# Dilated stage of a hybrid attention block: first units queued by hand, weighing steps tied to other points of the order

## The chip, the cores and the metric

One core of one Trainium2 chip runs the whole kernel. Its engines work side by side and are tied by semaphores: PE (TensorE, matmuls; PEld is its weight load), DVE (VectorE), ACT (ScalarE), POOL (GpSimd) and SP (SyncE, which here only issues DMAs). The metric is the device time of one execution in microseconds (us).

## The reference, cut to what matters

```python
h = rms_norm(x, g_pre)                       # x: 1024 tokens x 1024 channels
a_qkv, bq, bk, bv, mq, ga, gb, gm, mg = jnp.split(h @ w_in, split_at, axis=-1)
aq, ak, av = rope(q), rope(k), v             # of a_qkv, 24 heads of 64 channels
for gi, (window, dil) in enumerate(((128, 1), (512, 4), (2048, 16))):
    o_g, lse_g = dilated_window_attention(aq[gi's 8 heads], ak[...], av[...], window, dil)
wts = softmax(stack(lses), axis=0)           # over the three groups
oa = einsum('gbsh,gbshd->bshd', wts, stack(outs))
...                                          # ob: grouped-query attention, om: attention into a memory
ya = (oa * silu(ga)) @ w_br_a                # yb, ym likewise
gates = sigmoid(mg + b_merge)                # 3 x 1024 channels
merged = gates[0] * ya + gates[1] * yb + gates[2] * ym
out = x + rms_norm(merged @ w_out, g_post)
```

The change touches the dilated attention (the loop over `gi`), the weighted sum `oa` over its three groups, and the place at which that sum's last part is worked out, which lies in the stage that makes the arguments of `gates`.

## The kernel before, in words

All large products are computed as three products of split operands: a tensor is split into a high part (`A.activation(dst_h, src, AF.Copy)` on ACT, line 105) and a low part (a subtraction on DVE, line 106), and PE multiplies high by high, low by high and high by low.

A *unit* is one weight slab of 1024x128: `load_w` loads it (SP, line 114, tile `wr`) and splits it into `wh` and `wl` (two buffers of each). `dense` then runs 48 matmuls in two halves of 24, over 512 tokens each (lines 143, 145, 147), and each half goes to one of two PSUM banks (`d`). The function `evac` of the unit empties the bank. `run_items` prepares unit n+1 before it runs unit n, and `weave` mixes the matmuls of units with pieces of attention, by costs. On PE the order is the order of the program. On the other engines a scheduler orders the instructions by priority and dependences, save between `manual.__enter__()` and `manual.__exit__()`, where they too stand in the order of the program.

The stages that the change touches come in this order.

- **Values**, up to about 582 us: the values of the dilated heads, queued by hand on ACT, DVE, POOL and SP; each result is added on DVE (line 911, tile `vr`), scaled on ACT and stored.
- **Dilated stage**, about 582 to 1020 us. There are 12 items (p, g), four pairs of heads p by three groups g, two units each (query and key). `rope_half` empties a bank on DVE: four multiplications by the sine table into `t2a`, one of the whole bank by the cosine table into `t1a` (line 1050 for queries, 1049 for keys), and POOL adds both into `aq` or `ak` (line 1056). `weave(3)` runs the first three units alone. Then each item runs `plan`: eight steps T = 0..7. At each, `soft(T)` does the masked minimum on DVE (line 1135) and the exponentials on ACT (lines 1138, 1140, 1143); PE transposes the results of an earlier T (lines 1160, 1169), ACT copies them to SBUF (line 1172, tile `app`), and PE multiplies them by the values (line 1186). Scores for T = 0..3 and for T = 4..7 are made in two batches (line 1123), so that DVE works in two bursts of four T. `stats` (PE line 1205) transposes and stores minima and sums.
- **Weighing.** Once the three items of a pair of heads p are done, `combine` gives five steps: `fetch` (reads the statistics back), `weights` (some ten small DVE instructions and one on ACT, lines 1314 to 1325, then DMAs that write the weights and read them back as `wgt`), and `weigh(0)`, `weigh(1)`, `weigh(2)`: a multiplication on DVE over 128x1024 (line 1334, tile `og`), for the second and third also an addition on POOL (line 1338), and for the third a store (SP, line 1340). For p = 0, 1, 2 they go into the items (p+1, 0) and (p+1, 1): `combining(T)` takes the next step when T is the entry for it in `STEP_T`. `tc.issue_after(fp["last"].ins)` keeps the step behind the last `soft` or rope of that point.
- **Block stage**, 1020 to 1240 us, queued by hand: 11 pairs of gate slabs, each by seven products of blocks (12 matmuls each, `prod`), with block sums on POOL (line 1432, `sf`), their splits (`ch`, lines 105 and 106), and evacuations on DVE (lines 1455 and 1461, the latter a multiplication of SBUF by SBUF) and ACT (1462). `slot(n, i)` is the work queued beside product i of pair n. For p = 3 the table `COM` puts the five weighing steps into slots.

Of the kernel before, what the change touches and what calls it, by code (L numbers as in the profile page):

```python
# [50 lines left out]
def block(ctx: ExitStack, tc: tile.TileContext, x, xT, memT, cst, msk, bcst, tabA, gpost,  # L51
# [111 lines left out]
    def run_items(count):  # L163
        for _ in range(count):
            n = done[0]
            prepare(n)
            prepare(n + 1)
            yield from queue[n][1](ready.pop(n))
            done[0] += 1

    def cost_items(count):
        return sum(q[2] for q in queue[done[0]:done[0] + count])

    def weave(count, att=None, att_cost=0.0, lead=1.0, prio=ATT_PRIO):
        dg = run_items(count)
        dc = cost_items(count)
        d = a = 0.0
        live_d, live_a = True, att is not None
        while live_d or live_a:
            if live_d and (not live_a or a / att_cost >= min(1.0, d / dc * lead)):  # L180
                try:
                    d += next(dg)
                except StopIteration:
                    live_d = False
                    d = 1e18
            else:
                try:
                    with tc.high_priority(offset=prio):
                        a += next(att)
                except StopIteration:  # L190
                    live_a = False
# [3 lines left out]
    def add_unit(src, evac):  # L195
        def gen(w):
            for half in range(2):
                p = psd()
                yield from dense(w, half, p)
                evac(half, p)  # L200
        queue.append((lambda: load_w(src), gen, UNIT))
# [251 lines left out]
    ET = mybir.EngineType  # L453
    manual = tc.manual_schedule(engines={ET.Activation, ET.DVE, ET.Pool})
# [383 lines left out]
    manual = tc.manual_schedule(engines={ET.Activation, ET.DVE, ET.Pool, ET.SP})  # L838
# [181 lines left out]
    with tc.tile_pool(name="aa", bufs=1, reuse_waits="tile") as aa:  # L1020
# [19 lines left out]
        def rope_half(o, half, p, scale, g):  # L1040

            t = slice(half * 512, half * 512 + 512)
            t1 = ab.tile([P, 512], F32, name="t1a", bufs=3)
            t2 = ab.tile([P, 512], F32, name="t2a", bufs=3)
            cos, sin = tab[0][:, t], tab[1][:, t]

            def mult(out, x, y):
                if scale is None:
                    return V.tensor_tensor(out, x, y, op=OP.mult)  # L1049
                return V.scalar_tensor_tensor(out, x, scale, y, op0=OP.mult, op1=OP.mult)  # L1050

            for a in range(4):
                i, j = slice(32 * a, 32 * a + 32), slice(32 * (a ^ 1), 32 * (a ^ 1) + 32)
                mult(t2[i], p[j], sin[j])
            fp["last"] = mult(t1, p, cos)
            G.tensor_tensor(half_of(o, half, g), classes(t1, g), classes(t2, g), op=OP.add)  # L1056

        def add_a(p_, g):
            base = (p_ * 3 + g) * 2
            d = OPS[p_, g] = {}  # L1060

            def qk_evac(name, scale):
                def evac(half, p):
                    if half == 0:
                        d[name] = ab.tile([P, S], F32, name=f"a{name}", bufs=2)
                    rope_half(d[name], half, p, scale, g)
                return evac

            add_unit(wu[base], qk_evac("q", -0.125))
            add_unit(wu[base + 1], qk_evac("k", None))  # L1070
# [166 lines left out]
        def joined(*pieces):  # L1237
            pieces = [x for x in pieces if x]
            return (lambda: [fn() for fn, _ in pieces]), sum(c for _, c in pieces)

        def plan(it, pre, nxt):

            out = []

            def combining(T):
                if todo and T == STEP_T[-len(todo)]:
                    with tc.issue_after(fp["last"].ins):
                        todo.pop(0)()

            def tokens(T):  # L1250
                if T >= 2:
                    for nm, k in late[:2]:
                        with tc.issue_after(fp["last"].ins):
                            split_block(nm, k)
                    del late[:2]
                if T == 5:
                    token_tiles("T1", [ab.tile([P, S], R, name=f"a{c}", bufs=2) for c in "qk"])
                    load_block("T1", (0, 1))

            def ready():  # L1260
                if pre and pre["key"][1] == 2:
                    todo.extend(combine(pre["key"][0], [OG.pop((pre["key"][0], x)) for x in range(3)]))

            if it and not pre:
                out.append(it["scores"][0])
            for T in range(NT if it else 4):
                if T == 2 and pre:
                    out += [(lambda: None, 300.0), pre["stats"]]
                if it:
                    out.append(it["soft"][T])  # L1270
                out.append((lambda T=T: combining(T), 0.0))
                if it and not nxt:
                    out.append((lambda T=T: tokens(T), 0.0))
                if T < 2:
                    if pre:
                        out.append(pre["trans"][T + 6])
                elif it:
                    out.append(it["trans"][T - 2])
                if T == 3:
                    out.append(joined(pre and pre["pv"][1], it and it["scores"][1]))  # L1280
                    if it:
                        out.append((it["values"], 0.0))
                    if pre and it:
                        out.append((ready, 0.0))
                if T == 7:
                    out.append(joined(it["pv"][0], nxt and nxt["scores"][0]))
            return out
# [78 lines left out]
        def token_tiles(nm, tiles):  # L1366
            TB.setdefault(nm, []).extend([t[:, half[x]] for x in range(2)] for t in tiles)

        def load_block(nm, ks=range(4)):
            for k in ks:  # L1370
                nc.sync.dma_start(TB[nm][k][1].bitcast(F32), tsd[int(nm[1]) - 1, k])

        def split_block(nm, k):
            h, l = TB[nm][k]
            split(h, l, l.bitcast(F32))
# [1 line left out]
        late = []  # L1377

        todo = []
        STEP_T = (4, 6, 0, 2, 5)  # L1380
        seq = [(p_, g) for p_ in range(4) for g in range(3)]
        add_a(*seq[0])
        add_a(*seq[1])
        weave(3)
        items = [item(*x) for x in seq] + [None]
        for n in range(len(seq)):
            if n + 2 < len(seq):
# [25 lines left out]
    manual = tc.manual_schedule(engines={ET.Activation, ET.DVE, ET.Pool, ET.SP})  # L1413
# [20 lines left out]
    def block_of(n, nm):  # L1434
        src = part(n, 3) if nm == "A22" else SF[int(nm[1]) - 1]
        t = sr.tile([P, 2, 512], R, name="ch", bufs=5)
        split(t[:, 0], t[:, 1], src)
        BL[n][nm] = t[:, 0], t[:, 1]
# [81 lines left out]

    pre = {}
    com = combine(3, [OG.pop((3, x)) for x in range(3)])
    COM = {(0, 0): 0, (1, 1): 1, (2, 1): 2, (3, 1): 3, (4, 1): 4}

    def slot(n, i):

# [11 lines left out]
        if n < last:  # L1538
# [7 lines left out]
            elif i == 5:  # L1546
                weight_sum(n + 1, 4)
                block_of(n + 1, "S2")
        if (n, i) in COM:
            com[COM[n, i]]()  # L1550
        if (n, i) == (5, 0):
# [305 lines left out]
```

## Time and profile before

| what | value |
|---|---|
| time, median of 3 runs | 1458.5 us (1457.19 to 1459.48) |
| profiled execution: time | 1458.88 us |
| profiled execution: span from first to last instruction | 1457.1 us |
| mean granted TensorE clock | 0.995 |
| instructions | 20924 |

The profile lists instructions with the time at which they start, their duration and, in brackets, how long their engine had been idle and which instruction released it. A wait for several things is put down to the one that came last. A matmul of 512 columns starts about 0.23 us after the one before it while the shown duration is 0.39 us, because matmuls are pipelined; so distances between starts are what is to be read for PE.

### The profile page before, as it was taken

The page shows a single profiled execution, that of the slowest core. Times are in us where ns is not written, and L with a number is a line of the kernel's source. Part 1 is how long each engine was busy: PE and PEld are TensorE (multiplying, and loading weights), DVE is VectorE, ACT ScalarE, POOL GpSimd, SP SyncE. Part 2 cuts the span into 40 slices and gives each one's busy share as a digit, 9 for nine tenths or more (in the row PEclk, how much of TensorE's full clock was granted, in tenths as well). Part 3 has the DMA queues.
Part 4 walks back from the last instruction along what each step waited for, and adds up shares of the span by engine and source line. Part 5 has one row for each costly group of instructions (what it writes and reads, how often), then busy time and mean ns, then how long its engine had stood idle before and what let it go on. Part 6 is the DMA issues. An engine that isn't in the chain of part 4 may idle for free.

```text
span 1457.1 us, 20924 instructions
## 1 busy us (share of the span) xinstructions
PE 1423.2 (98%) x7548; PEld 1140.9 (78%) x7548; DVE 984.5 (68%) x1739; ACT 641.8 (44%) x1441; POOL 499.7 (34%) x382
## 2 busy tenths in 40 slices
PE   8999999999999999899999999999999999999998
PEld 7899986565666888687777778778787888888887
DVE  7665468776762367586687686873788787659643
ACT  6543365665554243145444544463534434212221
POOL 1415504666664420132232242230334331035322
PEclk9999999999999999999999999999999999999999
DMA  6332012232112675412131241342443443767122
GB/s 239 100 116 73 17 64 91 80 105 73 62 44 72 237 222 173 122 43 57 47 90 59 57 113 51 89 145 81 139 156 134 173 173 108 272 219 273 48 92 101
DMA packets 99448, 168.05 MB, mean 115 GB/s; under 512 B 21968, under 2 KB 51856, under 8 KB 99344
## 3 DMA queue, kind: packets, MB, share of 16 engines
q1 hardware_dynamic: 80192, 148.76, 31.7%
q10 hardware_dynamic: 19152, 17.96, 3.7%
q8 instruction: 59, 0.97, 0.3%
q14 instruction: 45, 0.37, 0.1%
HBM read 124.38 MB, written 42.30 MB: 114 GB/s over the span
## 4 chain that ended last, share of the span: by engine, by line
PE 76%; DVE 9%; ACT 5%; issue 5%; POOL 3%; DMA 2%; SPq 0%; ACTq 0%; POOLq 0%; DVEq 0%
PE s L125 9%; PE sc L125 9%; PE d L145 9%; PE d L143 8%; PE d L147 8%; PE s L967 6%; PE sc L1705 5%; PE ov L754 3%; PE d L967 2%; PE s L738 2%; PE tr L720 2%; PE s L739 2%; PE d L535 1%; PE tr L1186 1%; PE s L1123 1%
## 5 line engine op out<-in xcount | busy, mean ns | idle before, releaser
L143 PE MATMUL d<-hh,wh 128*128 128x512 f32 x672 | 271.2, 404 | 7.6 <-DVE t1a L1050 5.8
L147 PE MATMUL d<-hh,wl 128*128 128x512 f32 x672 | 269.4, 401 | 0.0
L145 PE MATMUL d<-hl,wh 128*128 128x512 f32 x672 | 269.4, 401 | 0.0
L105 ACT ACTIVATE wh<-wr 128x1024 fp32r<-128x1024 f32 (+1 forms) x79 | 72.2, 917 | 222.1 <-PE d L145 125.8
L143 PEld LDWEIGHTS d<-hh,wh 128*128 128x128 f32 x672 | 127.5, 190 | 38.0 <-issue 10.6
L145 PEld LDWEIGHTS d<-hl,wh 128*128 128x128 f32 x672 | 127.3, 189 | 31.3 <-issue 8.4
L147 PEld LDWEIGHTS d<-hh,wl 128*128 128x128 f32 x672 | 127.4, 190 | 29.1 <-issue 4.7
L745 POOL TENSOR_TENSOR bl<-bl,bp 128x512 f32<-128x512 f32 x96 | 131.5, 1370 | 53.6 <-ACT bp L741 48.1
L125 PE MATMUL sc<-hh,wh 128*128 128x512 f32 x384 | 118.4, 389 | 0.0
L106 DVE TENSOR_TENSOR wl<-wr,wh 128x1024 fp32r<-128x1024 f32 x53 | 74.6, 1409 | 37.5 <-ACT wh L105 37.1
L1056 POOL TENSOR_TENSOR aq<-t1a,t2a 128x512 f32<-128x512 f32 x24 | 44.7, 1862 | 160.7 <-DVE t1a L1050 149.4
L721 DVE TENSOR_REDUCE bn<-tr 128x1 f32<-128x512 f32 x128 | 86.1, 686 | 17.4 <-PE tr L720 16.1
L1049 DVE TENSOR_TENSOR t2a<-d,tab 32x512 f32<-32x512 f32 x96 | 66.0, 687 | 47.2 <-PE d L147 41.9
L741 ACT ACTIVATE bp<-s 128x512 f32<-128x512 f32 x128 | 75.9, 595 | 46.8 <-PE s L739 45.7
L1056 POOL TENSOR_TENSOR ak<-t1a,t2a 128x512 f32<-128x512 f32 x24 | 55.4, 2308 | 117.8 <-DVE t1a L1049 91.9
L125 PEld LDWEIGHTS sc<-hh,wh 128*128 128x128 f32 x384 | 72.1, 188 | 15.0
L1050 DVE SCALAR_TENSOR_TENSOR t2a<-d,tab 32x512 f32<-32x512 f32 x96 | 66.0, 687 | 25.8 <-PE d L147 24.0
L1432 POOL TENSOR_TENSOR sf<-wr 128x512 f32<-128x512 f32 x22 | 29.7, 1368 | 145.1 <-DVE ch L106 71.7
L1636 POOL TENSOR_TENSOR acc<-acc,th 128x1024 f32<-128x1024 f32 x15 | 40.9, 2729 | 112.0 <-DVE th L1635 109.3
L125 PE MATMUL sc<-hl,wh 128*128 128x512 f32 x192 | 74.7, 389 | 0.0
L1143 ACT ACTIVATE pra<-pra,sts 128x128 f32<-128x128 f32 (+2 forms) x152 | 66.4, 438 | 17.0 <-DVE sts L1135 17.0
L1135 DVE CUSTOM_DVE_ANT_0 pra<-s,mask 128x192 f32<-128x192 f32 (+2 forms) x192 | 56.1, 348 | 15.7 <-PE s L1123 14.9
(375 smaller groups left out, 3435.4 us busy)
## 6 DMA issues: line engine op xcount, KB each, us to landing
wr<-in_wu SPq DMA_DIRECT2D x64, 512.0 KB
th<-thd SPq DMA_DIRECT2D x24, 512.0 KB
thd<-rs ACTq DMA_DIRECT2D x44, 256.0 KB
g2d<-fth SPq DMA_DIRECT2D x24, 256.0 KB
vdr<-vr ACTq DMA_DIRECT2D x24, 256.0 KB
wgt<-wgd SPq DMA_DIRECT2D x24, 256.0 KB
ot<-od SPq DMA_DIRECT2D x12, 512.0 KB
wr<-in_wbr SPq DMA_DIRECT2D x24, 256.0 KB
```

The source lines that it names most:

```text
L105: A.activation(dst_h, src, AF.Copy)
L106: V.tensor_tensor(dst_l, src, dst_h.bitcast(F32), op=OP.subtract)
L125: PE.matmul(out_ps, a, b, start=i == 0, stop=i == n - 1)
L143: PE.matmul(dst, wh[:, k, :], hh[k][:, t], start=k == 0, stop=False)
L145: PE.matmul(dst, wh[:, k, :], hl[k][:, t], start=False, stop=False)
L147: PE.matmul(dst, wl[:, k, :], hh[k][:, t], start=False, stop=k == 7)
L721: fp["last"] = V.tensor_reduce(st[i]["n"][:, j, c:c + 1], s, axis=AX.X, op=OP.min)
L741: A.activation(pp, s, AF.Exp, scale=-1.0)
L745: G.tensor_tensor(lsum[i % 2], lsum[i % 2], pp, op=OP.add)
L967: PE.matmul(now[j], a, b, start=k == 0 and q == 0, stop=k == end and q == 2)
L1056: G.tensor_tensor(half_of(o, half, g), classes(t1, g), classes(t2, g), op=OP.add)
L1705: PE.matmul(parts[h], *terms[h][j], start=j == 0, stop=j == 23)
```

## The change

```diff
             def combining(T):
-                if todo and T == STEP_T[-len(todo)]:
+                while todo and T == STEP_T[-len(todo)]:
                     with tc.issue_after(fp["last"].ins):
                         todo.pop(0)()
...
         todo = []
-        STEP_T = (4, 6, 0, 2, 5)
+        STEP_T = (4, 7, 3, 3, 7)
         seq = [(p_, g) for p_ in range(4) for g in range(3)]
         add_a(*seq[0])
         add_a(*seq[1])
+        manual = tc.manual_schedule(engines={ET.Activation, ET.DVE, ET.Pool, ET.SP})
+        manual.__enter__()
         weave(3)
+        manual.__exit__(None, None, None)
...
-    COM = {(0, 0): 0, (1, 1): 1, (2, 1): 2, (3, 1): 3, (4, 1): 4}
+    COM = {(0, 0): 0, (1, 4): 1, (2, 4): 2, (3, 4): 3, (4, 4): 4}
```

Three things change. The first three units of the dilated stage stand in the order of the program on ACT, DVE, POOL and SP too. Within the items, `weights` goes from T = 6 to T = 7, `weigh(0)` from T = 0 and `weigh(1)` from T = 2 both to T = 3, and `weigh(2)` from T = 5 to T = 7; `while` lets two steps share one T. In the block stage the last four steps go from slot 1 to slot 4 of their pairs. PE has the same 5711 rows in the same order. SP keeps its order but for one weight load that stands two rows earlier and one store that stands behind two loads, both near the end of the dilated stage.

DVE at the start of the dilated stage: `vr` are the last additions of the values, `wl<-wr,wh` is the split of a weight slab, `t2a` and `t1a` are the rope of a bank.

```order
 L911 TENSOR_TENSOR vr<-s_5701,vy_4879 128x512
 L911 TENSOR_TENSOR vr<-s_5702,vy_4880 128x512
-L106 TENSOR_TENSOR wl<-wr,wh 128x1024
 L1050 SCALAR_TENSOR_TENSOR t2a<-d,tab_4850 32x512 x4
 L1050 SCALAR_TENSOR_TENSOR t1a<-d,tab_4849 128x512
 L1050 SCALAR_TENSOR_TENSOR t2a<-d,tab_4850 32x512 x4
 L1050 SCALAR_TENSOR_TENSOR t1a<-d,tab_4849 128x512
+L106 TENSOR_TENSOR wl<-wr,wh 128x1024
 L1049 TENSOR_TENSOR t2a<-d,tab_4850 32x512 x4
 L1049 TENSOR_TENSOR t1a<-d,tab_4849 128x512
```

The split of the third unit's slab moves from ahead of the first unit's two ropes to behind them.

DVE in the first burst (T = 0..3) of an item (p+1, 1), before: `pra` is the masked minimum, `og` a weighing.

```order
L1334 TENSOR_TENSOR og<-og,wgt 128x1024
L1135 ISA pra,sts<-s_7288,mask 128x192
L1135 ISA sts 128x1
L1135 ISA pra,sts<-s_7289,mask 128x192
L1135 ISA sts 128x1
L1050 SCALAR_TENSOR_TENSOR t2a<-d,tab_4850 32x512
L1050 SCALAR_TENSOR_TENSOR t1a<-d,tab_4849 128x512
L1049 TENSOR_TENSOR t2a<-d,tab_4850 32x512 x4
```

The same place after:

```order
L1050 SCALAR_TENSOR_TENSOR t2a<-d,tab_4850 32x512
L1050 SCALAR_TENSOR_TENSOR t1a<-d,tab_4849 128x512
L1135 ISA pra,sts<-s_7291,mask 128x192
L1135 ISA sts 128x1
L1135 ISA pra,sts<-s_7292,mask 128x192
L1135 ISA sts 128x1
L1334 TENSOR_TENSOR og<-og,wgt 128x1024 x2
L1049 TENSOR_TENSOR t2a<-d,tab_4850 32x512 x4
```

The two weighings, which stood behind the minima of T = 0 and of T = 2, stand together behind those of T = 3 and behind the rest of a query rope. On ACT the copy `app` that stood behind the exponentials of T = 1 now stands behind one more pair of exponentials.

DVE in the block stage at pair 4, before (`ch` are splits, `rs` and `sp` evacuations):

```order
L106 TENSOR_TENSOR ch<-wr,ch 128x512
L106 TENSOR_TENSOR ch<-sf_9949,ch 128x512
L1334 TENSOR_TENSOR og<-og,wgt 128x1024
L1455 TENSOR_TENSOR rs<-s_10457,sp_9952 128x512
L1461 TENSOR_TENSOR rs<-rs,rb 128x512
L106 TENSOR_TENSOR ch<-sf_9946,ch 128x512
```

One pair after the change (lines of the program behind the inserted ones are numbered three higher):

```order
L106 TENSOR_TENSOR ch<-sf_9951,ch 128x512
L1334 TENSOR_TENSOR og<-og,wgt 128x1024
L1458 TENSOR_TENSOR sp_9958<-s_10520,sp_9956 128x512
L106 TENSOR_TENSOR ch<-sf_9950,ch 128x512
L1458 TENSOR_TENSOR rs<-s_10543,sp_9957 128x512
L1464 TENSOR_TENSOR rs<-rs,rb 128x512
```

The weighing stood between the splits of S4 and S1 of its own pair (operands of products 4 and 5); it now stands between the splits of S3 and S2 of the next pair (operands of its products 3 and 2). POOL's block sum for S4 of the next pair stands behind the addition of that weighing.

## The prediction

> **What bounds the kernel now.** I read the busy table first, then the list of PE's own waits, then the timelines around those waits, and for the block stage a table by pairs.
>
> ```profile
> PE   1423.2 (98%) x7548; PEld 1140.9 (78%) x7548; DVE 984.5 (68%) x1739; ACT 641.8 (44%) x1441; POOL 499.7 (34%) x382
> ...
> PE d L143 <- DVE t1a L1050: 5.8, 1, 5.8
> PE tr L1205 <- ACT app L1172: 4.4, 6, 1.1
> PE tr L1160 <- ACT app L1172: 2.8, 4, 1.6
> PE s L125 <- DVE ch L106: 1.7, 2, 0.9
> ```
>
> PE is the bound, and its order does not change. So the time can move only by what PE waits, or by what clock it gets. These four groups (total us, times, longest) add up to 14.7 us of idle PE, and all of them lie where the change touches. What is not among them the change cannot win; what it makes later can be lost.
>
> **The first units (5.8 us of idle, and a slow clock behind it).**
>
> ```profile
> 582.69 0.39 PE L143 MATMUL d<-hh,wh 128*128 128x512 f32 x1
> 593.34 0.39 PE L147 MATMUL d<-hh,wl 128*128 128x512 f32 x1
> 599.53 0.76 PE L143 MATMUL d<-hh,wh 128*128 128x512 f32 x1 [5.80 <-DVE t1a L1050]
> 603.46 0.39 PE L143 MATMUL d<-hh,wh 128*128 128x512 f32 x1
> ...
> 599.50:603.40 3.90, 3.87 (x9) 0.50 0.00 0
> ...
> 587.97 0.69 DVE L911 TENSOR_TENSOR vr<-s,vy 128x512 f32<-128x512 f32 x1 [0.93 <-DMA vdr<-vr]
> 594.63 1.23 DVE L106 TENSOR_TENSOR wl<-wr,wh 128x1024 fp32r<-128x1024 f32 x1 [5.97 <-ACT wh L105]
> 595.89 2.79 DVE L1050 SCALAR_TENSOR_TENSOR t2a<-d,tab 32x512 f32<-32x512 f32 x4
> 598.69 0.69 DVE L1050 SCALAR_TENSOR_TENSOR t1a<-d,tab 128x512 f32<-128x512 f32 x1
> ...
> 593.54 1.06 ACT L105 ACTIVATE wh<-wr 128x1024 fp32r<-128x1024 f32 x1 [2.40 <-PE d L145]
> ```
>
> Unit 0 runs from 582.69 to 593.34, first and last of 48 matmuls: 10.65 / 47 = 0.2266 us from start to start. Its first bank was full at 582.69 + 23 x 0.2266 + 0.39 = 588.3, and DVE was free at 587.97 + 0.69 = 588.7. But the next instruction on DVE was the split of unit 2, which needs `wh` from ACT, which overwrites a buffer that unit 0 reads until 593.5. So DVE stood 5.97 us, the rope came after it, and PE waited 5.80 us for a bank. Then it ran at a granted clock of 0.50 for 3.90 us (the row of that stretch: length, busy PE and count, clock). From 593.34 to 603.46 there are ten starts where 10 x 0.2266 = 2.27 us would do: 10.12 - 2.27 = **7.85 us lost**.
>
> With the split behind both ropes: the first rope takes 588.7 + 2.79 + 0.69 = 592.2, and PE asks for that bank at 593.6, spare 1.4 us. The second bank is full at 593.7, its rope ends at 597.2, and PE asks for it at 593.57 + 24 x 0.2266 = 599.0, spare 1.8. The split then takes 597.2 to 598.4 and its unit starts at 593.57 + 10.88 = 604.4, spare 6.0. Queued behind that split are the two ropes of unit 1, of which the first bank fills only at 599.0, and SP's load into the freed `wr`, 2.6 us later than before, for unit 4, whose split waits for the end of unit 2 at 593.57 + 2 x 10.88 = 615.3, 17 us after that load is issued. The ends: 5.8 if only the idle goes, 7.85 with the clock. I take 7.85, since without the idle nothing in these rows slows the clock.
>
> **First burst of items (p+1, 1), three times.**
>
> ```profile
> 751.52 2.01 DVE L1334 TENSOR_TENSOR og<-og,wgt 128x1024 f32<-128x1024 f32 x1
> 753.44 0.35 DVE L1135 CUSTOM_DVE_ANT_0 pra<-s,mask 128x192 f32<-128x192 f32 x1
> 754.55 1.97 DVE L1334 TENSOR_TENSOR og<-og,wgt 128x1024 f32<-128x1024 f32 x1
> 759.03 1.38 DVE L1049 TENSOR_TENSOR t2a<-d,tab 32x512 f32<-32x512 f32 x2 [0.54 <-POOL og L1338]
> ...
> 753.90 0.46 ACT L1143 ACTIVATE pra<-pra,sts 128x192 f32<-128x192 f32 x1 [1.22 <-DVE sts L1135]
> 755.07 0.57 ACT L1172 ACTIVATE app<-tr 128x512 f32<-128x512 f32 x1
> 755.55 0.39 ACT L1138 ACTIVATE pra<-pra,sts 128x128 f32<-128x128 f32 x1
> 756.27 0.44 ACT L1143 ACTIVATE pra<-pra,sts 128x192 f32<-128x192 f32 x1
> ...
> 755.70 0.28 PE L1205 MATMUL tr<-cs,sts 128*32 128x128 f32 x1 [1.14 <-ACT app L1172]
> ```
>
> A weighing of 2 us stands between the minima of T = 0 and T = 1, so ACT starves for 1.22 us, its copy `app` ends late, and PE waits 1.14. Taken out of the burst, the 1.22 go; but ACT now does one more pair of exponentials ahead of that copy, 755.55 to 756.27 = 0.72. Net 0.5 us earlier, three times: **1.5 us**. Ends: 0 and 3 x 1.14 = 3.4. Behind the double weighing on DVE waits the rope of the key's first half. Four minima take from 753.44 to 754.55, 0.28 each, so the burst, two minima ahead of 751.52, begins at 751.0. It holds eight minima and the rest of the query rope (two operations, 1.4), then two weighings: 751.0 + 2.2 + 1.4 + 3.9 = 758.5, which is not later than the 759.03 at which that rope starts now. POOL's addition moves from ahead of the query's last `aq` addition to behind it; the 0.54 goes. `weights` at T = 7 ends where it ended, since the same instructions stand ahead of its last one, and its reader comes 3 us later than now.
>
> **Second burst of the same items.**
>
> ```profile
> 770.51 2.79 DVE L1334 TENSOR_TENSOR og<-og,wgt 128x1024 f32<-128x1024 f32 x1
> 776.68 2.79 DVE L1050 SCALAR_TENSOR_TENSOR t2a<-d,tab 32x512 f32<-32x512 f32 x4
> 773.67 0.40 ACT L1138 ACTIVATE pra<-pra,sts 128x128 f32<-128x128 f32 x1 [1.02 <-DVE sts L1135]
> 775.37 0.55 PE L1160 MATMUL tr<-cs,pra 128*128 128x128 f32 x3 [0.51 <-ACT app L1172]
> ...
> 956.11 2.06 POOL L1056 TENSOR_TENSOR ak<-t1a,t2a 128x512 f32<-128x512 f32 x1 [1.61 <-DVE t1a L1049]
> 961.86 2.97 POOL L1056 TENSOR_TENSOR ak<-t1a,t2a 128x512 f32<-128x512 f32 x1 [3.69 <-DVE t1a L1049]
> 964.86 0.63 ACT L105 ACTIVATE t2a<-t2a 128x512 fp32r<-128x512 f32 x1 [3.22 <-POOL ak L1056]
> 968.42 0.55 PE L1160 MATMUL tr<-cs,pra 128*128 128x128 f32 x3 [1.61 <-ACT app L1172]
> ```
>
> In the first two groups ACT starves 1.02 us for minima behind `weigh(2)` and PE then waits 0.51; ACT's order is the same there, so both 0.51 go. In the third, ACT first stands behind a split that waits for POOL's `ak`, which took 2.97 beside the weighing and 2.06 without one: 0.9 of the 1.61. Together **1.9 us**; ends 0 and 2.6. Behind `weigh(2)` wait the rest of `stats` and the next query rope, which starts at 776.68; the same instructions stand ahead of it in both orders, so it starts no later.
>
> **Block stage.**
>
> ```profile
> 1118.73:1137.77 19.04, 15.78 (x22) 1.00 0.36 114
> ...
> sum 98.00, PE 96.35; mean PE 19.27
> ...
> 1107.89 2.02 DVE L1334 TENSOR_TENSOR og<-og,wgt 128x1024 f32<-128x1024 f32 x1
> 1110.55 2.39 DVE L1461 TENSOR_TENSOR rs<-rs,rb 128x512 f32<-128x512 f32 x1
> 1112.86 0.68 DVE L106 TENSOR_TENSOR ch<-sf,ch 128x512 fp32r<-128x512 f32 x1
> 1109.99 2.40 POOL L1338 TENSOR_TENSOR og<-og 128x1024 f32<-128x1024 f32 x1 [9.96 <-DVE og L1334]
> 1113.59 0.50 PE L125 MATMUL s<-aq,ch 128*128 128x512 f32 x1 [0.73 <-DVE ch L106]
> ...
> 1143.79 0.69 DVE L106 TENSOR_TENSOR ch<-sf,ch 128x512 fp32r<-128x512 f32 x1 [1.48 <-ACT ch L105]
> ```
>
> The first row is a pair without weighing: 19.04 us, of which DVE is busy 15.78. The sum is over the five pairs from 1039.77 to it, the other four with a step each: 98.00 - 5 x 19.04 = 2.8 us too long. At 1113 the split of S1 is late by a weighing and by the `rs` beside POOL's addition (2.39 where 0.69 is usual). In slot 4 the weighing (2.0) and one blocked operation (1.7) delay the next pair's S4 split by up to 3.7 us. In the pair from 1137.77 that split ends at 1144.48, and product 4 needs it at 1137.77 + 4 x 2.72 + 0.45 = 1149.1, spare 4.6: no wait. I take **2.3** of 2.8, since part of pair 1 is the start of the stage. Ends: a gain of 2.8 and a loss of 1.5, if half the spare is missing in two pairs.
>
> The Trainium skill speaks against this place. "SBUF — State Buffer", section "SBUF: two separate sides", says that DVE with two SBUF inputs and POOL share one port pair that the first to start holds for its whole instruction. The 2.39 beside 2.40 agrees. By that rule alone the weighing in slot 4, among POOL's sums, would stand blocked, and the block term would be that of rival 2.
>
> **The sum**, against the profiled execution of 1458.88 (span 1457.1 and 1.8 around it): 7.85 + 1.5 + 1.9 + 2.3 = 13.55, so 1445.3. The median shown is 0.4 lower; I say **1445.0 us**.
>
> **Rivals.**
>
> 1. *Only the first units pay.* ACT's exponentials stay the limit in the bursts, and PE's waits move by a few transposes without shrinking. For it: ACT's order gets worse in the first burst. Against it: the idle brackets name DVE. 1458.5 - 7.85 = 1450.7, and up to 1453 with small new waits.
> 2. *The weighing is blocked by POOL's sums* in slot 4: it waits for a sum as `og` at 770.51 did (2.79 where 2.0 is usual) or longer, up to the 2.4 of an addition, on top of 3.7. That is 6.1 against a spare of 4.6, so 1.5 us lost in each of three pairs: the block term turns from -2.3 to +1.7 (the 2.8 gone, 4.5 new). 1449.0.
> 3. *The hand queue does not help:* the first rope is held by something else than the split, such as the memory that it takes over from the values stage. The 7.85 stay: 1452.8. Against it: before, it followed the split with no idle at all, and only POOL, PE and DVE hold it.
> 4. *Slower:* in the block stage the delay does not die out within a pair, since DVE has only some 3 us to spare in 19, so each weighed pair and the three after it lose. To decide it must eat 13.55 + 2.9, some 2.3 us in each of seven pairs. For it: the busy DVE. Against it: the pair from 1118.73 follows a weighed one and takes 19.04.
>
> **How the numbers follow.** Chances: forecast 0.66 (its own range 1442 to 1448.5), rival 1 0.13, rival 2 0.09, rival 3 0.06, rival 4 0.03, no change 0.03. The range reaches from all upper gains (7.85 + 3.4 + 2.6 + 2.8 = 16.7, so 1441.8) over rivals 1 and 2 to 1452. About 0.2% (2.9 us) is what a measurement can tell from no change. Rivals 1 to 3 all stay faster than that: faster 0.94, same 0.03, slower 0.03.
>
> **What would show it.** In the profile after: no idle of PE behind the first unit and a clock of 1.00 there; the split of unit 2 behind two query ropes; PE's waits on `app` at L1205 near 0.6 in three items and at L1160 gone in two; block pairs of 19.0 to 19.2 us. I am wrong if a new wait of PE on `t1a`, or on `ch` at the first matmuls of products 2 to 4, stands in the list.

## The result, and the profile after

| | before | after |
|---|---|---|
| median of the runs | 1458.65 us | 1449.26 us |
| ratio, 95% interval | | 0.9936 [0.9919, 0.9954] |
| span of the profiled execution | 1457.1 us | 1448.1 us |

The kernel became 9.4 us faster; 13.5 were forecast, and 1449.26 lies inside the range but 0.8 above the likeliest case's own. The sum hides two errors and one term that is right to 0.03 us, so the span has to be cut. Four instants of PE do it: the first matmul of unit 0, the first transposition at L1205 that PE waits for, and the starts of pair 0 and pair 6 of the block stage. These are rows of PE of the kernel before and then of the changed one (the block pairs' rows stand further down).

```profile
582.69 0.39 PE L143 MATMUL d<-hh,wh 128*128 128x512 f32 x1
721.80 0.28 PE L1205 MATMUL tr<-cs,sts 128*32 128x128 f32 x1 [0.34 <-ACT app L1172]
```
```profile
582.01 0.39 PE L143 MATMUL d<-hh,wh 128*128 128x512 f32 x1
713.24 0.28 PE L1205 MATMUL tr<-cs,sts 128*32 128x128 f32 x1 [0.34 <-ACT app L1172]
```

Between the two rows lie 139.11 us before and 131.23 after. In the same way for the rest; each stretch holds the same matmuls in the same order in both kernels. Pair 0 of the block stage starts at 1020.22 before and 1009.87 after, pair 6 at 1137.77 and 1128.77.

| stretch | before | after | difference | forecast |
|---|---|---|---|---|
| ahead of unit 0 (order unchanged) | 582.69 | 582.01 | -0.68 | 0 |
| unit 0 to the first wait at L1205 ("first units") | 139.11 | 131.23 | **-7.88** | -7.85 |
| first wait at L1205 to pair 0 ("bursts") | 298.42 | 296.63 | **-1.79** | -3.4 |
| pair 0 to pair 6 ("block stage") | 117.55 | 118.90 | **+1.35** | -2.3 |
| from pair 6 on | | | 0.00 | 0 |

The -0.68 is no work of the change: in the other kernels below unit 0 starts at 581.2 to 582.3, and nothing there was moved. One execution of the kernel e6_later took 2370.49 us at a granted clock of 0.557 and is left out of that kernel's median below.

The list of PE's own waits after (total us, times, longest):

```profile
PE tr L1205 <- ACT app L1172: 3.7, 6, 0.9
PE tr L1160 <- ACT app L1172: 2.4, 5, 1.7
...
PE s L125 <- ACT ch L105: 1.7, 3, 0.7
```

The wait on `t1a` is gone. The waits on `app` have shrunk by 1.1 us instead of 3.4. The wait on `ch` is a new one: three times, and it names ACT, where the old one named DVE.

**First units.** DVE after, and a table of PE by stretches (length; busy us and count of PE, PEld, DVE, ACT, POOL; granted clock; DMA):

```profile
588.37 2.79 DVE L1050 SCALAR_TENSOR_TENSOR t2a<-d,tab 32x512 f32<-32x512 f32 x4
591.18 0.69 DVE L1050 SCALAR_TENSOR_TENSOR t1a<-d,tab 128x512 f32<-128x512 f32 x1
593.09 2.79 DVE L1050 SCALAR_TENSOR_TENSOR t2a<-d,tab 32x512 f32<-32x512 f32 x4 [1.22 <-PE d L147]
...
596.50 1.22 DVE L106 TENSOR_TENSOR wl<-wr,wh 128x1024 fp32r<-128x1024 f32 x1
...
592.00:603.00 11.00, 11.00 (x50) 9.13 (x49) 8.02 (x11) 1.06 (x1) 4.30 (x3) 1.00 0.42 115
```

The split at 596.50 now stands behind both query ropes. The first rope ends at 591.87, where 592.2 was worked out. PE is busy for all of the 11 us, at a clock of 1.00. Both parts of the term came: the 5.80 of idle and the 2.05 of the slow clock behind it.

**Block stage**, table by pairs, 3 to 6, after:

```profile
1068.22:1088.56 20.34, 19.61 (x85) 15.61 (x84) 17.12 (x20) 8.02 (x12) 6.66 (x5) 1.00 0.43 130
1088.56:1108.72 20.16, 19.61 (x86) 15.61 (x84) 16.95 (x19) 7.39 (x11) 8.88 (x5) 1.00 0.42 131
1108.72:1128.77 20.05, 19.59 (x85) 15.61 (x84) 16.82 (x20) 7.39 (x11) 9.89 (x6) 1.00 0.38 131
1128.77:1147.81 19.04, 19.04 (x85) 15.77 (x84) 14.56 (x18) 7.38 (x11) 7.02 (x5) 1.00 0.46 167
```

Pair 1, which held `weights` and took 20.51, takes 19.34 now, pair 2 19.06; pair 0 is 0.4 longer than before. But the three pairs behind a weighing, 3 to 5, take 20.0 to 20.3, and DVE (fourth column) is busy for 17 us in them.

The 1.35 is the difference of two executions, and not all of it belongs to the slots. Pair 0, where no weighing was moved, takes 19.17 to 19.95 in the traces of this document, and 19.95 and 19.96 in two kernels with the slots of before (e2_steps, e11_slot1); its 0.40, after a wait of 0.46 for `hl`, is not the slots' doing. Pairs 1 to 5 take 98.00 before and 98.95 after. In four more traces with the slots of before they take 97.99 to 98.28 (e1_queue, e2_steps, e3_slot1, e11_slot1), in one more with the new slots 98.47 (e4_weights6). So the new slots cost some 0.2 to 1.0 us where a gain of 2.3 was forecast.

### The profile page after: what moved, and what is told of

The parts are those of the page before. It is cut to its first block, busy times and chain, and to the rows that moved or that the text cites. A ratio compares the mean times of both kernels' runs of the same rounds, so it can differ in the third digit from the quotient of the medians.

```text
span 1448.1 us, 20924 instructions
## 1 busy us (share of the span) xinstructions
PE 1420.2 (98%) x7548; PEld 1138.7 (79%) x7548; DVE 986.6 (68%) x1739; ACT 642.2 (44%) x1441; POOL 500.4 (35%) x382
## 4 chain that ended last, share of the span: by engine, by line
PE 78%; DVE 6%; ACT 5%; issue 4%; POOL 3%; DMA 3%; ACTq 0%; SPq 0%; POOLq 0%; DVEq 0%
PE d L145 9%; PE sc L125 9%; PE d L147 9%; PE d L143 9%; PE s L125 8%; PE s L967 6%; PE sc L1708 5%; PE ov L754 3%; PE tr L1186 2%; PE d L967 2%; PE s L1123 2%; PE s L738 2%; PE tr L720 2%; PE s L739 2%; PE d L535 2%
```

## Where the block stage lost

Rows of all engines of the changed kernel, around pair 3 (starts at 1068.22) and pair 4 (1088.56), in order of time:

```profile
1063.71 3.52 POOL L1435 TENSOR_TENSOR sf<-wr 128x512 f32<-128x512 f32 x2 [13.99 <-DMA wr<-in_wu]
...
1068.95 3.11 DVE L1334 TENSOR_TENSOR og<-og,wgt 128x1024 f32<-128x1024 f32 x1
...
1077.67 0.71 ACT L1465 ACTIVATE rs<-rs,hbm 128x512 f32<-128x512 f32 x1
1079.32 1.14 ACT L105 ACTIVATE ch<-sf 128x512 fp32r<-128x512 f32 x2
1079.99 0.50 PE L125 MATMUL s<-hh,ch 128*128 128x512 f32 x1 [0.73 <-ACT ch L105]
1080.71 0.30 PEld L125 LDWEIGHTS s<-hh,ch 128*128 128x128 f32 x2 [0.43 <-DVE ch L106]
...
1090.12 2.40 POOL L1338 TENSOR_TENSOR og<-og 128x1024 f32<-128x1024 f32 x1 [2.57 <-DVE og L1334]
1090.56 2.51 DVE L106 TENSOR_TENSOR ch<-sf,ch 128x512 fp32r<-128x512 f32 x1
1092.48 1.75 POOL L1435 TENSOR_TENSOR sf<-wr,sf 128x512 f32<-128x512 f32 x1
1094.25 4.79 SPq L1350 DMA_DIRECT2D wr<-in_wu  x2
```

Product 4 of pair 3 wants S4's first half from ACT and gets it late, 0.73 us, and then waits again for the second half from DVE, 0.43. ACT's copy stands behind the `tanh` of the pair before (and one evacuation), and these wait for DVE's `rs`, which is queued behind the weighing. That weighing took 3.11 among POOL's sums; the other two took 2.02. POOL's addition held a split of 0.7 for 2.51, as the prediction had it. One path more shows in the last two rows: POOL's last sum ends at 1094.23 (1092.48 + 1.75), and SP's load of the next `wr` goes out at 1094.25, because that sum frees its memory. The sum itself was not what S4 waited for in pair 4: it is S4's own, and ACT's copy of it began at 1099.48, over 5 us after its end. But an addition in front of the sum delays a load too, and POOL's next sums (`13.99 <-DMA wr` in the first row) wait for such a load.

How late DVE runs is read off one instruction: the start of its split of S4, counted from the start of the pair. These are its first and last rows of pairs 1 to 5 of the kernel before, and then its rows in pairs 1, 3 and 6 after:

```profile
1050.48 0.69 DVE L106 TENSOR_TENSOR ch<-sf,ch 128x512 fp32r<-128x512 f32 x1 [1.46 <-ACT ch L105]
...
1127.35 0.69 DVE L106 TENSOR_TENSOR ch<-sf,ch 128x512 fp32r<-128x512 f32 x1 [1.48 <-ACT ch L105]
```
```profile
1040.55 0.69 DVE L106 TENSOR_TENSOR ch<-sf,ch 128x512 fp32r<-128x512 f32 x1 [1.48 <-ACT ch L105]
...
1079.97 0.69 DVE L106 TENSOR_TENSOR ch<-sf,ch 128x512 fp32r<-128x512 f32 x1 [1.48 <-ACT ch L105]
...
1136.64 0.69 DVE L106 TENSOR_TENSOR ch<-sf,ch 128x512 fp32r<-128x512 f32 x1 [1.48 <-ACT ch L105]
```

Less the starts of their pairs, with the same reading of three experiments (in the last, pair 4's split shows no wait in front of it):

| start of S4's split in pair | 1 | 2 | 3 | 4 | 5 | 6 |
|---|---|---|---|---|---|---|
| before | 10.71 | 8.57 | 7.91 | 8.63 | 8.62 | 6.02 |
| after | 10.73 | 10.42 | 11.75 | 11.57 | 11.48 | 7.87 |
| later pairs (e6_later) | 10.72 | 10.39 | 9.19 | 9.12 | 10.25 | 11.27 |
| slot 2 (e9_slot2) | 10.73 | 10.44 | 9.55 | 11.25 | 12.15 | 7.86 |
| spread (e12_spread) | 10.73 | 10.46 | 9.58 | 7.45 | 8.00 | 9.70 |

PE waits wherever the number is over 11.0 (11.75 - 0.73 = 11.02, 11.57 - 0.55, 11.48 - 0.46). The stage begins at 10.7, with almost nothing to spare, and a pair without a weighing wins back 1.2 to 2.6 us. My spare of 4.6 was read in pair 6, where it is 11.0 - 6.0 and all lag has died out. In pairs 2 to 5 of before it was 2.4 to 3.1. The same row stood in each of those pairs.

## Experiments

Theory: the three parts add up, and what the block stage lost is a lag of DVE that is carried from pair to pair. Rivals: the parts meet in one shared state of DVE; or each weighing in slot 4 pays for itself, blocked by POOL's sums. All times stand against the kernel before on the same chip, whose median was 1458.0 to 1458.7 us. A difference below some 2.9 us is taken from the stretches of the traces, not from the medians.

**e1_queue: the hand-queued first units alone.**
```diff
+        manual = tc.manual_schedule(engines={ET.Activation, ET.DVE, ET.Pool, ET.SP})
+        manual.__enter__()
         weave(3)
+        manual.__exit__(None, None, None)
```


> The kernel before with the hand-queued first units alone. Theory (the parts add up): the 7.9 us that the trace after shows between the first unit and the items come here alone, 1458.7 - 7.9 = 1450.8 us; the waits for `app` stay at 1.14 and 0.51 and the block pairs keep their 19.43, 20.50, 19.04, 19.33, 20.08. Rival (part of the 7.9 belongs to the new step numbers): under 7 us.

Measured: 1449.71 us, ratio 0.9943 [0.993, 0.9957]. The stretch of the first units is 131.21, so -7.90; bursts 298.44 and block stage 117.45, as before. The rest of the gain in its trace lies ahead of unit 0 (581.20). The term belongs to this edit alone.

**e2_steps: the new step numbers alone.**
```diff
-                if todo and T == STEP_T[-len(todo)]:
+                while todo and T == STEP_T[-len(todo)]:
...
-        STEP_T = (4, 6, 0, 2, 5)
+        STEP_T = (4, 7, 3, 3, 7)
```


> The kernel before with the new step numbers and the repeated `while` alone. Theory (the bursts gave what the trace after shows): 0.7 + 1.1 = 1.8 us, 1456.9 us, with a wait of 0.9 at L1205 and a new one of 0.2 at L1160. Rival (the bursts give the prediction's 1.5 + 1.9, and something else in the changed kernel ate the difference): 1455.3 us, with waits of 0.6 at L1205.

Measured: 1456.41 us, ratio 0.9987 [0.9978, 0.9995]. Bursts 296.59, so -1.83; the first units stay at 139.12, with the 5.80. The bursts gave what the trace after shows, and nothing else ate the difference: my terms for them were too large.

**e3_slot1: the changed kernel, block stage as before.**
```diff
-    COM = {(0, 0): 0, (1, 4): 1, (2, 4): 2, (3, 4): 3, (4, 4): 4}
+    COM = {(0, 0): 0, (1, 1): 1, (2, 1): 2, (3, 1): 3, (4, 1): 4}
```


> The changed kernel with the weighings of the block pairs back at slot 1. Theory (the new place itself costs): the three waits of PE on `ch` go, the pairs return to the lengths of before, 1449.3 - 1.35 = 1447.9 us. Rival (the block pairs suffer from the state in which the bursts leave DVE): the waits on `ch` stay, 1449.3 us.

Measured: 1447.90 us, ratio 0.993 [0.9917, 0.9942]; block stage 117.43, pairs 1 to 5 of 20.53, 19.04, 19.30, 20.08 and 19.04. The three waits are gone, so the new slot itself costs what pairs 1 to 5 lost, 0.96 us against this trace; the other 0.5 of the stage's 1.47 is pair 0.

**e4_weights6: the changed kernel with `weights` at T = 6.** The trace after showed why the first burst gave little. DVE rows of the changed kernel, and then of this one, around `weights` and the first minimum of the burst:

```profile
732.15 2.15 DVE L1320 TENSOR_TENSOR cdn<-ceg,cpt 128x48 f32<-128x48 f32 x1
...
735.04 0.21 DVE L1325 TENSOR_TENSOR ceg<-ceg,cds 128x48 f32<-128x48 f32 x1
...
742.79 0.36 DVE L1135 CUSTOM_DVE_ANT_0 pra<-s,mask 128x192 f32<-128x192 f32 x1
```
```profile
732.57 1.87 DVE L1325 TENSOR_TENSOR ceg<-ceg,cds 128x48 f32<-128x48 f32 x1
...
741.98 0.36 DVE L1135 CUSTOM_DVE_ANT_0 pra<-s,mask 128x192 f32<-128x192 f32 x1
```

One small operation of `weights` meets POOL's `ak` (from 730.99 for 3.25 after, from 731.17 for 3.21 here) and stands for about 2 us. At T = 7 it is the fifth-last of them (2.15, where 0.21 is usual), and four more come behind it; at T = 6, as before the change, it is the last (1.87). So the rope and the burst behind them start 0.4 later against PE.
```diff
-        STEP_T = (4, 7, 3, 3, 7)
+        STEP_T = (4, 6, 3, 3, 7)
```


> The changed kernel with `weights` back at T = 6 (the numbers 4, 6, 3, 3, 7). Theory (the burst's first minimum comes 0.4 us late because the moved small operations end 0.4 later behind POOL's `ak`): the first minimum comes 0.4 us earlier against PE in all three items, the waits at L1205 fall from 0.9 to 0.5, 1449.3 - 1.2 = 1448.1 us. Rival (ACT's eight pairs of exponentials ahead of the copy set the wait, not DVE): it stays at 0.9, 1449.3 us.

Measured: 1447.65 us, ratio 0.9927 [0.9915, 0.994]; bursts 295.47, 1.16 less than after, and PE's row in the first item:

```profile
746.12 0.28 PE L1205 MATMUL tr<-cs,sts 128*32 128x128 f32 x1 [0.53 <-ACT app L1172]
```

The wait is 0.52 to 0.53 in the three items, where it was 0.9. The rival falls: ACT's order is the same in both kernels.

**e5_noadd: no additions of the fourth pair of heads on POOL.** This kernel leaves out the shares of the second and the third group there, so it is an experiment only.
```diff
-                if g:
+                if g and p_ < 3:
                     G.tensor_tensor(ogs[0], ogs[0], ogs[g], op=OP.add)
```


> The changed kernel without POOL's two additions of the fourth pair of heads (its output lacks the shares of the second and the third group of dilations there); the weighings stay. Theory (a lag of DVE that is carried from pair to pair): the start of the split of S4, counted from the start of its pair, is the measure; in the changed kernel it is 10.42, 11.75, 11.57, 11.48 us in pairs 2 to 5, and PE waits where it is over 11.0. A free pair wins back some 2.2 to 2.6. Pair 3 keeps its 0.73, since no addition lies ahead of it; in pairs 4 and 5 the delay falls from about 4 to 2.0 to 2.4, less than what is won back, so their waits go: 1449.3 - 2.1 = 1447.2 us. Rival (the weighings themselves, or POOL's own sums, hold the split): all three waits stay, 1449.3 us.

Measured: 1447.79 us, ratio 0.9929 [0.9916, 0.9942]. Pairs 3 to 5:

```profile
1067.53:1087.27 19.74, 19.61 (x85) 15.61 (x84) 16.51 (x20) 7.71 (x12) 7.17 (x5) 1.00 0.40 134
1087.27:1106.34 19.07, 19.07 (x85) 15.77 (x84) 14.58 (x19) 7.39 (x11) 6.07 (x5) 1.00 0.52 166
1106.34:1125.64 19.30, 19.30 (x86) 15.66 (x84) 16.08 (x20) 7.38 (x11) 6.74 (x5) 1.00 0.33 109
```

Pairs 4 and 5 are within 0.26 of 19.04, with all weighings in place, although each of the three took 3.10 to 3.11 among POOL's sums here. Block stage 116.13, 2.8 less than after. The rival falls. Pair 3, expected to keep all of its wait, fell from 20.34 to 19.74. The 0.6 is not the edit's; it shows in POOL's sums in pair 2:

```profile
1062.41 3.53 POOL L1435 TENSOR_TENSOR sf<-wr 128x512 f32<-128x512 f32 x2 [13.35 <-DMA wr<-in_wu]
```

They start 13.93 into the pair, where after they start 14.55 into it (1063.71), while SP's loads went out at the same point of the pair in both (1054.20 and 1054.86, both 5.7 into it). So a load landed 0.6 later after (the sums start 14.18 into the pair in e4_weights6 and 14.51 in e6_later, up to there with the same work on these engines); the split of a slab on DVE beside these sums took 2.23 instead of 1.59, and S4's split of pair 3 comes at 11.15 here and at 11.75 after. So 0.6 of what pair 3 lost hangs on when a load lands, which differs from one execution to the next.

**e6_later: the weighings one pair later.**
```diff
-    COM = {(0, 0): 0, (1, 4): 1, (2, 4): 2, (3, 4): 3, (4, 4): 4}
+    COM = {(0, 0): 0, (1, 4): 1, (3, 4): 2, (4, 4): 3, (5, 4): 4}
...
-        if (n, i) == (5, 0):
+        if (n, i) == (6, 0):
```


> The changed kernel with the three weighings one pair later (pairs 3, 4 and 5 in place of 2, 3 and 4; their memory is given back at pair 6 and not 5). The same weighings, additions and loads, in the same slot. Theory (lag carried over): pair 3, free now, brings the split of S4 from 10.4 to about 8.2 us; behind the first weighing it stays there; then 9.8, then 11.4: no waits in pairs 3 to 5, at most 0.4 in pair 6; 1449.3 - 3.0 = 1446.3 us, and at worst 1447. Rival (each weighed pair pays for itself, by the weighing blocked behind POOL's sums and the splits behind POOL's addition): three waits again, one pair later, 1449.3 us.

Measured: 1448.26 us, ratio 0.9932 [0.9919, 0.9945]. Pairs 3 to 5 ran free, 19.04 each, as the lag has it and the rival has not. But pairs 6 and 7 took 19.85 and 20.34, with waits on `ch` of 0.25 and 0.73, so that the nine pairs from 0 to 8 are only 1.5 us shorter than after (174.51 against 176.02). POOL and SP there:

```profile
1128.40 1.74 POOL L1435 TENSOR_TENSOR sf<-wr,sf 128x512 f32<-128x512 f32 x1
1141.93 2.53 POOL L1435 TENSOR_TENSOR sf<-wr 128x512 f32<-128x512 f32 x2 [11.79 <-DMA wr<-in_wu]
```
```profile
1130.16 0.33 SPq L1350 DMA_DIRECT2D wr<-in_wu  x1
```

The sum that frees `wr` ends at 1130.14, late behind the addition; the load goes out at 1130.16, 5.4 us into the pair (0.6 in pair 6 after, at 1129.41), and POOL's next sums wait for it till 1141.93. Pair 6 was expected to wait up to 0.4, but pair 7 was not: DVE stood 3.00 us there for the copy of a late sum. This is the second path, and my expectation had left it out. From pair 6 on loads of `ot` and `gt` share the queue, and a DVE operation of 2.3 us is added to each pair, which leaves less to win back with.

**e7_pool: the products on POOL, slot 1 of pairs 3 to 5.**
```diff
-                V.tensor_tensor(ogv, ogv, wv, op=OP.mult)
+                (G if p_ == 3 else V).tensor_tensor(ogv, ogv, wv, op=OP.mult)
```
with slots (3, 1), (4, 1), (5, 1) for the weighings.

> The changed kernel with the three products of the fourth pair of heads on POOL and not on DVE, in slot 1 of pairs 3, 4 and 5, where POOL stands idle for some 10 us. Theory (lag carried over, and DVE with two inputs in memory stands still while POOL works): DVE no longer spends 2.0 us on a weighing, but is held up to 2.4 by POOL's product and up to 2.4 by its addition; the delay is 2 to 4 us a pair, about that of the weighing on DVE, and the lag has room since pair 3 begins at 8.2: 1446 to 1447.5 us. Rival (POOL and DVE do not hold each other): the splits stay at about 6 to 8 us, no waits at all, 1445.9 us, and no operation of DVE near 2.4 us beside POOL's product. Rival (POOL's sums behind it come late): waits on `sf` or `ch` in slots 4 and 5, over 1449 us.

Measured: 1448.78 us, ratio 0.9941 [0.9928, 0.9954]; pairs 3 to 5 of 19.65, 19.92, 20.47. POOL and DVE in pair 5:

```profile
1108.34 3.39 POOL L1334 TENSOR_TENSOR og<-og,wgt 128x1024 f32<-128x1024 f32 x1
1111.81 2.73 POOL L1338 TENSOR_TENSOR og<-og 128x1024 f32<-128x1024 f32 x1
```
```profile
1109.56 2.73 DVE L1464 TENSOR_TENSOR rs<-rs,rb 128x512 f32<-128x512 f32 x1
1112.20 0.68 DVE L1458 TENSOR_TENSOR rs<-s,sp 128x512 f32<-128x512 f32 x1
1112.91 2.18 DVE L1464 TENSOR_TENSOR rs<-rs,rb 128x512 f32<-128x512 f32 x1
```

The product takes 3.39 on POOL where DVE needs 2.0. An `rs` of 0.69 with both inputs in SBUF stands until POOL's instruction ends, twice, while the `rs` that reads a PSUM tile takes its usual 0.68 in between. So DVE loses 2.0 + 1.5 us and saves 2.0 and the 1.8 of the blocked split: no gain to speak of, and the time is 1.3 above the range that I gave. That they hold each other agrees with the Trainium skill, "SBUF — State Buffer", section "SBUF: two separate sides". The rival in which they do not hold each other falls.

**e8_both: e4 and e6 together.**


> The changed kernel with both corrections: the step numbers 4, 6, 3, 3, 7, and the three weighings of the block stage one pair later. Theory: the gains add, 1.6 (measured for the step numbers) and 3.0 (expected for the later pairs): 1449.3 - 4.6 = 1444.7 us, faster than both kernels. Rival (the waits in the pairs come by the state in which the bursts leave DVE, so that the gains overlap): 1446 to 1447.5 us.

Measured: 1447.45 us, ratio 0.9927 [0.9915, 0.9939]. Bursts 295.52: that gain is there. The block pairs lose again in 6 and 7 (20.32, 20.29), as in e6, so the time is some 2.8 above my theory's and inside the rival's range. The rival's cause does not show: pairs 1 to 4 take 19.33, 19.07, 19.04 and 19.04 here and 19.33, 19.06, 19.04 and 19.04 in e6, whatever the bursts left. Why pairs 5 and 6 lose 0.8 more here than in e6 stays open.

**e9_slot2, e10_all2, e11_slot1: e4 with other slots.**
```diff
-    COM = {(0, 0): 0, (1, 4): 1, (2, 4): 2, (3, 4): 3, (4, 4): 4}
+    COM = {(0, 0): 0, (1, 4): 1, (2, 2): 2, (3, 2): 3, (4, 2): 4}    # e9_slot2
+    COM = {(0, 0): 0, (1, 2): 1, (2, 2): 2, (3, 2): 3, (4, 2): 4}    # e10_all2
+    COM = {(0, 0): 0, (1, 1): 1, (2, 1): 2, (3, 1): 3, (4, 1): 4}    # e11_slot1
```


> The changed kernel with the step numbers 4, 6, 3, 3, 7 and the three weighings of the block stage in slot 2 of pairs 2, 3 and 4, behind the split of S1; `weights` stays in slot 4 of pair 1. Theory (lag carried over): the start of the split of S4 is 10.7 us in pair 1; a pair wins back 2.6, `weights` takes 2.4, a weighing alone 2.0, one with its addition 3.8. So 10.4, 9.8, 11.0, 12 in pairs 2 to 5; PE waits where it is over 11.0, so only in pair 5, about 1 us; and none at S1, whose split now stands ahead of the weighing. Block pairs 2 to 5: 1 us too long and not 3.5: 1447.65 - 2.5 = 1445.2 us. Rival (POOL's addition, now ahead of its sums, makes these late, and they set the splits of S3 and S2): new waits on `ch` at products 2 and 3, 1447.6 us or more.

Measured: 1446.99 us, ratio 0.9924 [0.9912, 0.9937]. The split of S4 came at 10.44, 9.55, 11.25 and 12.15, where 10.4, 9.8, 11.0 and 12 were forecast: the model of the lag holds to 0.3 us. Its price did not: pairs 4 and 5 took 19.83 and 20.73, 2.5 us too long and not 1, since PE waits for each half of a late split and not once (1.13 and 0.43 in pair 5).

> As the last one, but `weights` too in slot 2 (of pair 1). Theory (lag carried over): `weights` no longer stands between POOL's sums, where its first small operation took 1.26 in place of 0.17, so it costs 1 us less of DVE's time: pairs 2 to 5 at 9.4, 8.8, 10, 11.2: no wait over 0.2; 1444.5 us. Rival (the small operations wait for ACT's exponential in slot 2, and the split of the next pair's own blocks behind them is late): a wait of 0.5 to 1.5 us at the start of pair 2, 1445.5 to 1447 us.

Measured: 1447.35 us, ratio 0.9926 [0.9912, 0.994]. The rival's wait came; PE at the start of pair 2:

```profile
1049.01 0.50 PE L125 MATMUL s<-hh,wl 128*128 128x512 f32 x1 [1.23 <-DVE wl L106]
```

Its cause is only in small part the rival's: DVE waited 0.31 us for ACT's exponential, but four of the small operations took 0.94 to 1.30 beside POOL's sums, where 0.17 to 0.21 is usual. So the premise of my theory was wrong, that slot 2 of pair 1 is clear of these sums. Pair 5 took 20.43 as well, with S4's split at 11.80 where 11.2 was forecast.

> The changed kernel with the step numbers 4, 6, 3, 3, 7 and the block stage as it was before the change (slot 1). Theory (the parts add up): 1.6 us from the one and 1.35 from the other, each measured alone: 1449.3 - 2.95 = 1446.3 us, waits at L1205 of 0.53 and two waits on `ch` at S1 of 0.92 and 0.73. Rival (they overlap, because both gains come from the state of DVE at the start of the block stage): 1447.6 us.

Measured: 1447.02 us, ratio 0.9924 [0.9912, 0.9937]. Bursts 295.47, block stage 118.01 where e3 had 117.43; the 0.6 is in pair 0 (19.96 against 19.44). So the parts add up but for that.

**e12_spread: e4, with the weighings spread over pairs 2, 4 and 5.**
```diff
-    COM = {(0, 0): 0, (1, 4): 1, (2, 4): 2, (3, 4): 3, (4, 4): 4}
+    COM = {(0, 0): 0, (1, 4): 1, (2, 2): 2, (4, 0): 3, (5, 2): 4}
...
-        if (n, i) == (5, 0):
+        if (n, i) == (6, 0):
```


> The changed kernel with the step numbers 4, 6, 3, 3, 7 and the weighings of the block stage spread: `weights` in slot 4 of pair 1, the weighings in slot 2 of pair 2, slot 0 of pair 4 and slot 2 of pair 5 (memory given back at pair 6). Theory (lag carried over, with the steps that the last runs measured: a free pair wins back 2.6, a weighing with its addition adds 3.8 to 4.3 before that): the split of S4 starts at 10.4, 9.6, 10.8, 8.2, 9.9 us in pairs 2 to 6 and up to 11.4 in pair 7, so at most one wait of 0.4; 1.5 to 2 us less than with slot 2 of pairs 2, 3 and 4: 1445.2 us. Rival (a shortage that only moves, as when all three stood one pair later: loads and sums that come late behind the addition, and POOL waiting for them): waits of 0.5 to 1 in pairs 6 and 7, 1446.5 to 1447 us.

Measured: 1445.73 us, ratio 0.9908 [0.9892, 0.9925], the lowest median of all, though its interval overlaps those of the last three; the trace is what tells them apart. Pairs 3 and 4:

```profile
1067.82:1086.86 19.04, 19.04 (x86) 15.77 (x84) 15.74 (x20) 8.06 (x13) 8.64 (x6) 1.00 0.34 111
1086.86:1105.90 19.04, 19.04 (x86) 15.77 (x84) 14.80 (x18) 7.40 (x11) 7.81 (x5) 1.00 0.40 139
```

No wait on `ch` is left; pairs 3 to 8 take 19.04 each, and the block stage 115.25: 2.30 less than before, 3.65 less than after. The splits came as forecast in pairs 2, 3, 5 and 6, and in pair 4 at 7.45 instead of 10.8:

```profile
1091.74 0.69 DVE L106 TENSOR_TENSOR ch<-wr,ch 128x512 fp32r<-128x512 f32 x1 [0.56 <-ACT ch L105]
1092.35 2.05 DVE L1334 TENSOR_TENSOR og<-og,wgt 128x1024 f32<-128x1024 f32 x1
1094.31 0.69 DVE L106 TENSOR_TENSOR ch<-sf,ch 128x512 fp32r<-128x512 f32 x1
```

In slot 0 the weighing stands where DVE otherwise idles 1.48 us for ACT's copy, so it costs some 0.6 and not 2.0, and its addition on POOL (1094.48) comes behind the split. (This kernel has one small wait of 0.37 that the others lack, at unit 1 of the first units.)

## Why the prediction was right or wrong, point by point

The time lies inside the range because the largest term was right and the range was wide. Of the three terms one came as forecast, one came at half its size and one with the wrong sign; the last two are off by 5.3 us together, and the 0.68 ahead of unit 0 that made up for some of it was luck.

- **First units, -7.85: right** (-7.88, and -7.90 alone). Rival 3 fell. Counting the slow clock with the idle was right.
- **First burst, -1.5: the size failed**, at the sentence "`weights` at T = 7 ends where it ended". It ended 0.4 later, since another of its small operations met POOL's `ak`. The stretch from a wait of 0.34 at L1205 to the transpositions at L1160 behind the longer wait there holds a first burst: in the first item 35.43 before (721.80 to 757.23), 35.32 after (713.24 to 748.56) and 34.92 with `weights` at T = 6. Over the three items that is 0.37 us gained after and 1.51 with T = 6, so the mechanism and its 0.5 an item were right. A second step was wrong too, and cost nothing that PE shows: the double weighing was counted as 3.9 and took 5.41 (from 746.43, its first half held by POOL's `aq` of 746.05), so the key's rope started at 751.88, 1.4 later against PE than before.
- **Second burst, -1.9: half of it failed.** The two 0.51 went, and each was worth 0.73 to 0.74 (61.28 from those transpositions to the next wait of 0.34 before, 60.55 after). The 0.9 of the third item was never the weighing's: nothing was gained there (0.05 lost), so the term came to -1.42. Rows after, the weighing now behind all eight minima:

```profile
951.47 3.00 POOL L1056 TENSOR_TENSOR ak<-t1a,t2a 128x512 f32<-128x512 f32 x1 [2.18 <-DVE t1a L1049]
...
954.50 0.64 ACT L105 ACTIVATE t2a<-t2a 128x512 fp32r<-128x512 f32 x1 [3.26 <-POOL ak L1056]
...
954.66 2.02 DVE L1334 TENSOR_TENSOR og<-og,wgt 128x1024 f32<-128x1024 f32 x1
...
958.07 0.55 PE L1160 MATMUL tr<-cs,pra 128*128 128x128 f32 x3 [1.65 <-ACT app L1172]
```

  `ak` takes 3.00 with no weighing beside it. What stands beside it in both kernels is the split of a weight slab on DVE (`wl`, 951.31 for 1.22 after, 961.70 for 1.22 before), which fits the 0.9, though no run here takes it away. The weighing before was the one that was held, not the one that held:

```profile
963.94 2.79 DVE L1334 TENSOR_TENSOR og<-og,wgt 128x1024 f32<-128x1024 f32 x1
```
- **Block stage, -2.3: the sign failed**, at the step "spare 4.6: no wait". The spare was that of pair 6; in pairs 2 to 5 it is 2.4 to 3.1, and the stage begins with 0.3. Rival 2 named this place, the three pairs and their 1.5 each, and its price (+1.7, measured +1.35 with pair 0 and +0.95 without) was nearer than the forecast. But it came out so for a wrong spare (6.1 against 4.6), and its cause came in one pair of three: one weighing was held by POOL's sums (3.11), the other two were not (2.02). Rival 4's mechanism, a lag that does not die out within a pair, is what was at work, at 3.65 us against the forecast (0.40 of it in pair 0) and not the 16.4 at which it decides. The evidence that I set against it, the clean pair from 1118.73, shows that PE did not wait there, not that DVE had caught up: the split stands at 8.62 in that pair. The 2.3 themselves were to be had: spreading the weighings gives 2.30.

## What to carry to other kernels

A spare is to be read in the very stretch into which the work is moved, as the position of the operand's last instruction against the start of each round, round by round: a round with no wait can still be late, and a late round hands its lag on. Work for a nearly full engine is best spread over rounds and put where that engine idles for another one; three pieces in three neighbouring rounds cost 3.4 us here, the same three spread cost nothing. And a chain of small operations is to be moved with an eye on which of them will stand beside a long instruction of POOL: one of 0.2 took some 2 us there.

## What the runs showed of the hardware

- POOL's addition of 128x1024 took 2.35 to 2.40 us (2.73 in e7_pool, where DVE was still at work as it started), its product of the same size 3.38 to 3.39, beside 2.0 for the product on DVE.
- Beside such an instruction of POOL, DVE's instruction with both inputs in SBUF took 2.18 to 2.73 instead of 0.69; those that read a PSUM tile kept their 0.68.
- After 5.8 us of idle PE ran at a granted clock of 0.50 for 3.9 us; without the idle, 1.00. What had looked like 5.8 us was worth 7.9.
